# The end of an attention item: its addition, its copies of the reciprocal sums and GpSimd's three operations queued behind the next parts

## The chip, the cores and the metric

The kernel runs on one core of a Trainium2 chip. The metric is the device time of one execution in microseconds. The profile names the engines PE (TensorE's matmuls), PEld (its weight loads), DVE (VectorE), ACT (ScalarE), POOL (GpSimd) and SP (SyncE, which issues the DMAs here).

## The reference

One layer over 1024 latent tokens and 256 context tokens, width 1024, in fp32:

```python
x = macaron half-step SwiGLU(x)                  # every sub-layer with RMSNorm, shift, scale and gate
o_na  = neighbourhood attention(q, k, v, ...)    # 8 heads of 64; 8 x 16 window of a 64-wide grid + 256 context keys
o_mla = latent attention(q, k, v)                # 8 heads; 1024 latent + 256 context keys
y = g_na * (o_na @ w_o_na) + g_mla * (o_mla @ w_o_mla)
x = residual(x, y @ w_out)
x = macaron half-step SwiGLU(x)
```

Each attention is a softmax over scores, times the values:

```python
s = jnp.einsum('bqhd,bkhd->bhqk', q * q.shape[-1] ** -0.5, k).astype(jnp.float32)
p = jax.nn.softmax(s, axis=-1).astype(v.dtype)
return jnp.einsum('bhqk,bkhd->bqhd', p, v)
```

The neighbourhood attention adds a relative bias to its local scores, and puts local and context scores into one softmax.

## The kernel before

The change lies in the attention, which takes 1347 to 1757 us of the profiled execution. It is a list of 64 items, `todo`: 32 neighbourhood items (8 heads x 4 column blocks, `NaItem`), then 32 MLA items (8 heads x 4 blocks of 256 queries, `MlaItem`). Item n has 256 queries of one head. An fp32 operand of a product is kept as a pair, a rounded high half and the rest, so that a product is two or three matmuls.

For one item:

- `scores` multiplies queries by keys into PSUM banks of the kind "s" (tile `bs`). DVE adds the bias or copies, with the maximum (L1802 and L1777), and reduces the maxima (L1809, MLA L1909). ACT's exponential (L1811, MLA L1913) works in place and leaves the sums; DVE takes their reciprocal (L1815, MLA L1917). With an odd item, `widen` (L1769, POOL) spreads the reciprocals of this item and of the even one before it over a tile, `rope` in the profile.
- `values` gives the parts: three in a neighbourhood item (local, context, edge), five in an MLA item. A part transposes its exponentials on PE into a bank of the kind "m" (tile `bm`), ACT casts them to the high half (L1835, MLA L1939), DVE subtracts for the low half (L1836, MLA L1940). What is returned, `w`, are the part's matmuls with the values into the item's bank of the kind "v" (tile `bv`, columns 0 to 255). There are two "v" banks, so item n+2 writes the bank of item n.
- The `w` of the last part ends with `head_out`. A matmul with the values gives 128 rows, of which two blocks of 64 are to be added. In an even item, PE first transposes the widened reciprocals into columns 256 to 511 of the same bank, for this item and for the next: ACT copies them to `rb` (L1749) and to `other`, which the odd item takes as its `rb` (L1750). Then ACT copies one block to `o` (L1753), DVE adds the other (L1754), POOL multiplies by `rb` (L1755), casts (L1757) and subtracts (L1758) for the pair in `ona` or `omla`.

The loop over n makes a part, appends its `w` to `pending`, runs a share of the exponentials and reciprocals of an earlier item (`soft`), some steps of the scores of item n+3 (`ahead`), and the oldest `w` once more than two are pending (`LAG`). The matmuls, transposes and loads (helpers at L120, L132, L154 and L157) keep the order in which the program is written. The instructions of `head_out`, `turned`, `part` and `scores` on ACT, DVE and POOL go through no helper, and the framework's scheduler places them; each engine then runs its queue in that order. The small tiles `t`, with `o` and `rb` in them, come from a pool of 12 buffers in turn.

Of the kernel before, what the change touches and what calls it, by code (L numbers as in the profile page):

```python
# [12 lines left out]
ALU = mybir.AluOpType  # L13
# [25 lines left out]
def f32(ap):  # L39
    return ap.bitcast(F32)  # L40
# [3 lines left out]
def hybrid_block(ctx: ExitStack, tc: tile.TileContext, a: dict, out: bass.AP):  # L44
    nc = tc.nc
# [30 lines left out]
    def T2(dt=F32, n=512):  # L76
        return pools["t"].tile([P, n], dt, tag="t", name=nm("t"))
# [78 lines left out]
    def turn_(o, x, i):  # L156
        return pin(nc.tensor.transpose(o, x, i))  # L157
# [929 lines left out]
    o = len(plan.main)  # L1087
# [93 lines left out]
    o = d1_at + 4 * NP  # L1181
# [9 lines left out]
    for f, x in ups:  # L1191
        o = len(plan.main)
# [5 lines left out]
    for e in range(2):  # L1198
        for f in range(NF):
            o = len(plan.main)  # L1200
# [71 lines left out]
    def emit_cq(i, ci, x, bank):  # L1272

        t, q = x, T2()
        if bank:
            t = T2()
            act.copy(t, x)
        act.activation(q, t, AF.Square)
        if ci in sq:
            vec.tensor_tensor(sq[ci], sq[ci], q, op=ALU.add)  # L1280
        else:
            sq[ci] = q
        store(cqx[i, :, ci * 512:(ci + 1) * 512], t)
# [22 lines left out]
    for p in range(3):  # L1306
        punits.append(Unit(h2, [cq_src(2 * p), cq_src(2 * p + 1)],
                           lambda i, ci, x, bank, p=p: emit_cq(2 * p + i, ci, x, bank)))

    o = len(plan.main)  # L1310
# [147 lines left out]
    o = len(plan.main)  # L1458
# [5 lines left out]
    for x, (c, s, ts) in enumerate(sets):  # L1464
        o = len(plan.main)
# [239 lines left out]
    o = va_at  # L1705
# [8 lines left out]
    o = len(plan.main)  # L1714
# [3 lines left out]
    o = len(plan.main)  # L1718
# [3 lines left out]
    o = len(plan.main)  # L1722
# [4 lines left out]
    o = len(plan.main)  # L1727
# [9 lines left out]
    def head_out(pv, n, h, hi, lo, shape):  # L1737

        b, c = (0, 64) if h % 2 == 0 else (64, 0)
        t = T2()
        o, rb = t[b:b + 64, :256], t[b:b + 64, 256:512]
        if n % 2 == 0:
            for i in range(2):
                turn_(pv[:, 256 + i * P:256 + (i + 1) * P], wide(n)[:, i * P:(i + 1) * P], ident)
            other = held[0] = T2()
            nc.scalar.copy(rb, pv[0:64, 256:512])  # L1749
            nc.scalar.copy(other[b:b + 64, :256], pv[64:128, 256:512])  # L1750
        else:
            rb = held[0][b:b + 64, :256]
        nc.scalar.copy(o, pv[c:c + 64, :256])  # L1753
        nc.vector.tensor_tensor(o, o, pv[b:b + 64, :256], op=ALU.add)  # L1754
        nc.gpsimd.tensor_tensor(o, o, rb, op=ALU.mult)  # L1755
        o = shape(o)
        nc.gpsimd.tensor_copy(hi[b:b + 64], o)  # L1757
        nc.gpsimd.tensor_tensor(lo[b:b + 64], o, f32(hi[b:b + 64]), op=ALU.subtract)  # L1758

    sums, held = {}, [None]  # L1760

    def wide(n):

        return rope.rearrange("p a b -> p (a b)")[:, (n // 2) % 2 * 256:(n // 2) % 2 * 256 + 256]
# [18 lines left out]
    class NaItem:  # L1783
# [37 lines left out]
        def values(self):  # L1821
# [35 lines left out]
            def edge():  # L1857
                eh, el = edges[(h * 4 + j) % 2]
                turned(((0, 0), (1, 2)), eh, el)

                def w():
                    weigh(pv[0], vt(0), [x[:, 0:256] for x in (eh, el)], False, False)
                    weigh(pv[0], vt(3), [x[:, 128:384] for x in (eh, el)], False, True)
                    hi, lo = [o.rearrange("p (s r j c) -> p s r j c", s=2, r=8, j=4)[:, :, :, j, :] for o in ona[h // 2]]
                    head_out(pv[0], self.n, h, hi, lo, lambda t: t.rearrange("p (s r c) -> p s r c", s=2, r=8))
                return w
# [20 lines left out]
    class MlaItem:  # L1887
# [39 lines left out]
        def values(self):  # L1927
            hd, b, prl, prc, h = self.head, self.b, self.prl, self.prc, self.head.h
            pv = []

            def part(g):
                pb = PB("m")
                for x in range(2):
                    for s in range(2):
                        kb = 2 * g + x
                        src = prl[s][:, kb * P:(kb + 1) * P] if g < 4 else prc[:, s * 256 + x * P:s * 256 + (x + 1) * P]
                        turn_(pb[:, (2 * x + s) * P:(2 * x + s + 1) * P], src, ident)
                t = (T2(F32R), T2(F32R))
                nc.scalar.copy(t[0], pb)  # L1939
                nc.vector.tensor_tensor(t[1], pb, f32(t[0]), op=ALU.subtract)  # L1940

                def w():
                    if g == 0:
                        pv.append(PB("v"))
                    for x in range(2):
                        kb = 2 * g + x
                        vt = hd.v[:, kb * P:(kb + 1) * P] if g < 4 else hd.kvc[:, 512 + x * P:512 + (x + 1) * P]
                        weigh(pv[0], vt, [y[:, x * 256:(x + 1) * 256] for y in t], kb == 0, kb == 9)
                    if g == 4:
                        hi, lo = [o[:, b * 256:(b + 1) * 256] for o in omla[h // 2]]  # L1950
                        head_out(pv[0], self.n, h, hi, lo, lambda t: t)
                return w

            return [lambda g=g: part(g) for g in range(5)]

    soft, started, todo, edges, pending = [], [], [], [], []
    AHEAD, LAG, EARLY = 3, 2, 2

    def start(n):

        if n < len(todo):
            it = todo[n]()
            started.append(it)
            yield from it.scores()
# [101 lines left out]
    for n in range(len(todo)):  # L2066
        ahead = chain(start(EARLY), start(AHEAD)) if n == 0 else start(n + AHEAD)
        if n in (last - 4, last - 2):
            fm.load(int(n == last - 2))
        if n in (last - 3, last - 1):  # L2070
            fm.split()
        parts = led_parts[n] if n in led_parts else started[n].values()
        many = len(parts)
        soft_n = list(soft)
        for x, part in enumerate(parts):
            pending.append(part())
            take = rare[n][x] if n in rare else -(-len(soft_n) // (many - x))
            for f in soft_n[:take]:
                soft.remove(f)
                f()  # L2080
            del soft_n[:take]
            for _ in range(5 // many if n else 3):
                next(ahead, None)
            if x in fill.get(n, ()):
                fm.step()
            if len(pending) > LAG:
                pending.pop(0)()
        for _ in ahead:
            pass
    while pending:  # L2090
        pending.pop(0)()
    while fm.left:
        fm.step()
    pinned[0] = False
# [48 lines left out]
    for d in range(KD):  # L2143
        o = len(plan.main)
# [37 lines left out]
    o = len(plan.main)  # L2182
# [13 lines left out]
    o = len(plan.main)  # L2196
# [67 lines left out]
    for j in range(4):  # L2264
        o = d2_at + 5 * NP + 2 * j
        for x, i in enumerate((-2, 0, 1)):
            plan.spread([lambda j=j, x=x: done2(j, x)], o + i, o + i + 1)
        o = e - 9 + j
        plan.spread([lambda j=j: done_half(4 + j, 1)], o, o + 1)
        o = e - 4 + j  # L2270
# [83 lines left out]
```

## Time and profile before

| | before |
|---|---|
| median of 3 runs | 2560.17 us (2557.73 to 2561.82) |
| profiled execution | 2559.68 us, span 2557.7 us, mean granted clock 0.998 |
| PE, DVE, ACT, POOL busy | 2527.3, 1936.3, 1259.2, 217.8 us |
| 1375.36 to 1462.02 us (neighbourhood items): PE, DVE, ACT, POOL | 86.24, 84.43, 81.50, 44.93 of 86.66 us |
| 1564 to 1716 us (MLA items) | 151.29, 128.05, 121.26, 36.91 of 152 us |
| copies `rb`, `other` and `o` (L1749, L1750, L1753) | 32, 32 and 64 of them, medians 363, 368 and 368 ns |
| addition (L1754) | 64, median 420 ns |
| POOL's product, cast, subtraction (L1755, L1757, L1758) | 64 each, means 732, 398 and 733 ns |

How to read it: the span runs from the first to the last instruction of one profiled execution. A row of the timeline has the start, the length, engine, line, operation, output and inputs, and in brackets how long the engine had stood and what ended that. Consecutive matmuls overlap in the pipeline, so the sum of their lengths is more than their distance. Releasers are inferred.

### The profile page before, as it was taken

To read this page: it belongs to the slowest core of one execution; us is meant where nothing else is said; L and a number is where in the kernel's file an instruction comes from. 1 tells how busy PE (TensorE), PEld (TensorE's weight loads), DVE (VectorE), ACT (ScalarE), POOL (GpSimd) and SP (SyncE) were. 2 spreads that over 40 slices of the span, in tenths; PEclk is the share of its full clock that TensorE was granted. 3 is DMA by queue.
4 is the path that set the end of the run, shared out by engine and by line. 5 is a ranking of instruction groups with operands and counts; after the bars stand their busy time and mean duration, and the time that the engine had idled before them with its cause. 6 is when DMAs were issued, how large, how long until landed. Compare 5 with 4: busy or idle time off the path is not lost. (4 is left out here: it accounts for less than half of the span.)

```text
span 2557.7 us, 38230 instructions
## 1 busy us (share of the span) xinstructions
PE 2527.3 (99%) x13416; PEld 2158.7 (84%) x13416; DVE 1936.3 (76%) x3629; ACT 1259.2 (49%) x2375; POOL 217.8 (9%) x372
## 2 busy tenths in 40 slices
PE   8999999999999999999999999999999999999998
PEld 6888888888998888889888999998888888888887
DVE  4789986887786577874568988887886888767777
ACT  5632223445654653433447987783266322233444
POOL 1000000001000000001003522221011000000003
PEclk9999999999999999999999999999999999999999
DMA  8455543943674666755978733207836445326724
GB/s 307 157 173 195 195 151 117 345 137 132 231 274 138 215 230 225 241 184 176 301 280 275 241 94 76 65 11 262 296 123 216 156 157 169 111 99 233 273 70 165
DMA packets 245760, 479.47 MB, mean 187 GB/s; under 512 B 30464, under 2 KB 71616, under 8 KB 245568
## 3 DMA queue, kind: packets, MB, share of 16 engines
q1 hardware_dynamic: 245568, 477.02, 55.4%
q8 instruction: 106, 1.74, 0.3%
q14 instruction: 86, 0.70, 0.1%
HBM read 348.93 MB, written 127.99 MB: 186 GB/s over the span
## 5 line engine op out<-in xcount | busy, mean ns | idle before, releaser
L120 ACT CAST xu<-t 128x512 fp32r<-128x512 f32 (+1 forms) x270 | 161.0, 601 | 494.4 <-DVE t L120 352.6
L154 PE MATMUL bm<-xu,xu 128*128 128x512 f32 (+2 forms) x1572 | 366.6, 386 | 0.0
L154 PE MATMUL bs<-xv,xu 128*128 128x512 f32 x1488 | 357.3, 389 | 0.3 <-DVE t L120 0.3
L154 PEld LDWEIGHTS bm<-xu,xu 128*128 128x128 f32 x1572 | 288.1, 188 | 56.7
L154 PE MATMUL bv<-xv,xu 128*128 128x512 f32 x1342 | 335.4, 389 | 0.0
L154 PEld LDWEIGHTS bs<-xv,xu 128*128 128x128 f32 x1488 | 279.1, 188 | 59.0 <-issue 1.1
L154 PEld LDWEIGHTS bv<-xv,xu 128*128 128x128 f32 x1342 | 251.8, 188 | 52.3
L154 PE MATMUL bs<-xv,xv 128*128 128x512 f32 x1086 | 265.8, 390 | 0.0
L120 DVE TENSOR_TENSOR xu<-xu,xu 128x512 fp32r<-128x512 f32 (+1 forms) x296 | 201.7, 686 | 55.2 <-ACT xu L120 54.9
L154 PEld LDWEIGHTS bs<-xv,xv 128*128 128x128 f32 x1086 | 203.0, 188 | 41.7
L154 PE MATMUL bs<-xu,xu 128*128 128x512 f32 (+1 forms) x972 | 226.2, 382 | 0.0
L120 DVE TENSOR_TENSOR t<-t,t 128x512 f32<-128x512 f32 (+2 forms) x278 | 185.1, 673 | 45.0 <-ACT t L120 36.0
L154 PE MATMUL bs<-w,w 96*128 96x512 f32 (+3 forms) x832 | 206.5, 367 | 4.7 <-DVE st L1802 4.0
L154 PEld LDWEIGHTS bs<-xu,xu 128*128 128x128 f32 x972 | 177.4, 188 | 35.7 <-issue 1.4
L120 POOL TENSOR_SCALAR st<-st 128x1 f32<-128x1 f32 (+1 forms) x66 | 33.5, 508 | 1887.4 <-ACT t L120 1869.2
L120 ACT CAST xv<-t 128x512 fp32r<-128x512 f32 x170 | 105.8, 622 | 169.8 <-PE bv L154 69.0
L120 DVE TENSOR_TENSOR xu<-t,xu 128x512 fp32r<-128x512 f32 (+1 forms) x270 | 179.0, 663 | 10.7 <-ACT xu L120 10.6
L154 PE MATMUL bm<-xv,xv 128*128 128x512 f32 x690 | 182.8, 390 | 0.0
L120 ACT CAST xu<-xu 128x512 fp32r<-128x512 f32 x218 | 132.7, 618 | 71.3 <-DMA xu<-in_wo 43.6
L120 DVE TENSOR_TENSOR xv<-t,xv 128x512 fp32r<-128x512 f32 x170 | 116.6, 686 | 65.6 <-ACT xv L120 56.5
L154 PE MATMUL bv<-t,w 128*128 128x256 f32 x896 | 150.9, 288 | 2.0 <-DVE t L1940 1.5
L154 PEld LDWEIGHTS bm<-xv,xv 128*128 128x128 f32 x690 | 129.2, 188 | 27.1 <-issue 0.4
(242 smaller groups left out, 4229.3 us busy)
## 6 DMA issues: line engine op xcount, KB each, us to landing
d<-t SPq DMA_DIRECT2D x366, 256.0 KB, 2.6
t<-d SPq DMA_DIRECT2D x274, 256.0 KB, 3.8
xu<-in_f1w SPq DMA_DIRECT2D x59, 512.0 KB, 4.2
xu<-in_f2w SPq DMA_DIRECT2D x58, 512.0 KB, 3.7
t<-in_wada SPq DMA_DIRECT2D x112, 256.0 KB, 5.1
xv<-in_f1w SPq DMA_DIRECT2D x44, 512.0 KB, 7.4
xu<-in_winT SPq DMA_DIRECT2D x38, 512.0 KB, 4.8
w<-d SPq DMA_DIRECT2D x32, 512.0 KB, 6.4
```

Source lines behind the costliest of these rows:

```text
L120: return lambda *x, **y: pin(f(*x, **y))
L154: return pin(nc.tensor.matmul(o, s, m, start=start, stop=stop, skip_group_check=open_group[0]))
```

## The change

`head_out` still has PE transpose the reciprocals and ACT copy `o`. The rest goes into a function `one` that is appended to a list, `late`; an even item appends the copy to `other` as a second entry. The loop takes one entry out of `late` after each new part, ahead of that part's share of exponentials. So the addition, the copy to `rb` (now behind the addition) and POOL's three operations are written behind the transposes, cast and subtraction of the next part, and the copy to `other` behind those of the part after that. What is left runs after the loop. The lines move: 1753 to 1752 (`o`), 1754 to 1755 (addition), 1749 to 1757 (`rb`), 1750 to 1765 (`other`), 1755, 1757 and 1758 to 1758, 1760 and 1761 (POOL); everything behind them by 7.

```diff
         t = T2()
         o, rb = t[b:b + 64, :256], t[b:b + 64, 256:512]
-        if n % 2 == 0:
+        even = n % 2 == 0
+        if even:
             for i in range(2):
                 turn_(pv[:, 256 + i * P:256 + (i + 1) * P], wide(n)[:, i * P:(i + 1) * P], ident)
             other = held[0] = T2()
-            nc.scalar.copy(rb, pv[0:64, 256:512])
-            nc.scalar.copy(other[b:b + 64, :256], pv[64:128, 256:512])
         else:
             rb = held[0][b:b + 64, :256]
         nc.scalar.copy(o, pv[c:c + 64, :256])
-        nc.vector.tensor_tensor(o, o, pv[b:b + 64, :256], op=ALU.add)
-        nc.gpsimd.tensor_tensor(o, o, rb, op=ALU.mult)
-        o = shape(o)
-        nc.gpsimd.tensor_copy(hi[b:b + 64], o)
-        nc.gpsimd.tensor_tensor(lo[b:b + 64], o, f32(hi[b:b + 64]), op=ALU.subtract)
+
+        def one():
+            nc.vector.tensor_tensor(o, o, pv[b:b + 64, :256], op=ALU.add)
+            if even:
+                nc.scalar.copy(rb, pv[0:64, 256:512])
+            nc.gpsimd.tensor_tensor(o, o, rb, op=ALU.mult)
+            x = shape(o)
+            nc.gpsimd.tensor_copy(hi[b:b + 64], x)
+            nc.gpsimd.tensor_tensor(lo[b:b + 64], x, f32(hi[b:b + 64]), op=ALU.subtract)
+
+        late.append(one)
+        if even:
+            late.append(lambda: nc.scalar.copy(other[b:b + 64, :256], pv[64:128, 256:512]))
...
             pending.append(part())
+            if late:
+                late.pop(0)()
...
     while pending:
         pending.pop(0)()
+    while late:
+        late.pop(0)()
```

PE and SP run the same instructions in the same order before and after. ACT's queue at the end of an even MLA item (the one whose copies start at 1597.68 us in the profile), before; COPY on L1749, L1750 and L1753 are `rb`, `other` and `o`, CAST a part's high half, ACTIVATE an exponential, and the numbers in the names tell buffers and uses apart:

```order
L1913 ACTIVATE xu_16906,st_16904<-xu_16906,st_16903 128x1024
L1749 COPY t_17074<-bv_16960 64x256
L1750 COPY t_17077<-bv_16960 64x256
L1753 COPY t_17074<-bv_16960 64x256
L1939 CAST t_17090<-bm_17085 128x512
L1913 ACTIVATE t_16907,st_16904<-t_16907,st_16903 128x256
L1939 CAST t_17110<-bm_17105 128x512
L1939 CAST t_17129<-bm_17124 128x512
L1939 CAST t_17151<-bm_17146 128x512
```

and after, where L1752, L1757 and L1765 are `o`, `rb` and `other`:

```order
L1920 ACTIVATE xu_16906,st_16904<-xu_16906,st_16903 128x1024
L1752 COPY t_17074<-bv_16960 64x256
L1946 CAST t_17084<-bm_17079 128x512
L1920 ACTIVATE t_16907,st_16904<-t_16907,st_16903 128x256
L1946 CAST t_17109<-bm_17104 128x512
L1757 COPY t_17074<-bv_16960 64x256
L1765 COPY t_17077<-bv_16960 64x256
L1946 CAST t_17129<-bm_17124 128x512
L1946 CAST t_17151<-bm_17146 128x512
```

`o` stands straight behind the exponential, and the two other copies stand behind the casts of two parts.

DVE's queue at the same place, before (TENSOR_SCALAR copies scores with their maximum, the TENSOR_TENSOR that writes 128x512 is a part's low half, L1754 the addition):

```order
L1777 TENSOR_SCALAR xu_17040,st_17036<-bs_17065 128x512
L1777 TENSOR_SCALAR xu_17040,st_17036<-bs_17095 128x512
L1754 TENSOR_TENSOR t_17074<-t_17074,bv_16960 64x256
L1940 TENSOR_TENSOR t_17091<-bm_17085,t_17090 128x512
L1777 TENSOR_SCALAR xu_17041,st_17036<-bs_17115 128x512
L1940 TENSOR_TENSOR t_17111<-bm_17105,t_17110 128x512
```

and after, where the addition is L1755:

```order
L1784 TENSOR_SCALAR xu_17040,st_17036<-bs_17065 128x512
L1784 TENSOR_SCALAR xu_17040,st_17036<-bs_17094 128x512
L1947 TENSOR_TENSOR t_17085<-bm_17079,t_17084 128x512
L1755 TENSOR_TENSOR t_17074<-t_17074,bv_16960 64x256
L1947 TENSOR_TENSOR t_17110<-bm_17104,t_17109 128x512
L1784 TENSOR_SCALAR xu_17041,st_17036<-bs_17115 128x512
```

The addition has changed places with the low half of the part that follows.

ACT's queue at the end of an even neighbourhood item (its copies start at 1414.27 us in the profile), before; `xu<-bm` is the cast of an edge part, `xu,st` an exponential:

```order
L1749 COPY t_14152<-bv_14097 64x256
L1750 COPY t_14155<-bv_14097 64x256
L1753 COPY t_14152<-bv_14097 64x256
L1835 CAST xu_13012<-bm_14163 128x2x128
L1835 CAST t_14175<-bm_14177 128x512
L1811 ACTIVATE xu_14113,st_14117<-xu_14113,st_14116 128x640
L1835 CAST t_14201<-bm_14203 128x512
L1811 ACTIVATE xu_14114,st_14117<-xu_14114,st_14116 128x640
L1753 COPY t_14224<-bv_14170 64x256
```

and after:

```order
L1752 COPY t_14152<-bv_14097 64x256
L1842 CAST xu_13012<-bm_14157 128x2x128
L1842 CAST t_14174<-bm_14176 128x512
L1818 ACTIVATE xu_14113,st_14117<-xu_14113,st_14116 128x640
L1757 COPY t_14152<-bv_14097 64x256
L1765 COPY t_14155<-bv_14097 64x256
L1842 CAST t_14201<-bm_14203 128x512
L1818 ACTIVATE xu_14114,st_14117<-xu_14114,st_14116 128x640
L1752 COPY t_14224<-bv_14169 64x256
```

The two copies have moved from the front, ahead of `o`, to behind the first exponential. On DVE the same place reads, before:

```order
L1777 TENSOR_SCALAR xu_14114,st_14115<-bs_14112 128x256
L1754 TENSOR_TENSOR t_14152<-t_14152,bv_14097 64x256
L1809 TENSOR_REDUCE st_14116<-st_14115 128x2
L1836 TENSOR_TENSOR xu_13012<-bm_14163,xu_13012 128x2x128
L1815 RECIPROCAL st_13979<-st_14051 128x2
L1836 TENSOR_TENSOR t_14176<-bm_14177,t_14175 128x512
```

and after:

```order
L1784 TENSOR_SCALAR xu_14114,st_14115<-bs_14112 128x256
L1843 TENSOR_TENSOR xu_13012<-bm_14157,xu_13012 128x2x128
L1816 TENSOR_REDUCE st_14116<-st_14115 128x2
L1755 TENSOR_TENSOR t_14152<-t_14152,bv_14097 64x256
L1822 RECIPROCAL st_13979<-st_14051 128x2
L1843 TENSOR_TENSOR t_14175<-bm_14176,t_14174 128x512
```

The reduction of the maxima (TENSOR_REDUCE) stood behind the addition; now it stands behind the edge part's subtraction (`xu<-bm,xu`), and the addition behind it. In the first pair of items, ACT's queue reads, after:

```order
L1752 COPY t_13128<-bv_12919 64x256
L1842 CAST t_13133<-bm_13135 128x512
L1818 ACTIVATE xu_13045,st_13049<-xu_13045,st_13048 128x640
L1818 ACTIVATE xu_13046,st_13049<-xu_13046,st_13048 128x640
L1757 COPY t_13128<-bv_12919 64x256
L1818 ACTIVATE xu_13089,st_13093<-xu_13089,st_13092 128x640
L1842 CAST t_13164<-bm_13166 128x512
L1818 ACTIVATE xu_13090,st_13093<-xu_13090,st_13092 128x640
L1765 COPY t_13131<-bv_12919 64x256
L1752 COPY t_13188<-bv_13110 64x256
```

There `other` (L1765) stands behind four exponentials; before, both copies stood ahead of `o` here as well.

More of the change, by code (lines that the diff above doesn't have):

```diff
@@ L1954, in values @@
             return [lambda g=g: part(g) for g in range(5)]
-    soft, started, todo, edges, pending = [], [], [], [], []
+    soft, started, todo, edges, pending, late = [], [], [], [], [], []
     AHEAD, LAG, EARLY = 3, 2, 2
```

## The prediction

> **What bounds the kernel now.** I read the page first, then the busy time by stretch, then the waits of the attention stretch, and last the timeline at the ends of single items. The page's first part:
>
> ```profile
> PE 2527.3 (99%) x13416; PEld 2158.7 (84%) x13416; DVE 1936.3 (76%) x3629; ACT 1259.2 (49%) x2375; POOL 217.8 (9%) x372
> ```
>
> PE has work for all but 30 us of the 2557.7 us span, so the order of the other engines can only pay through PE's stalls. The busy time by stretch (window, its length, then PE, PEld, DVE, ACT, POOL, granted clock, DMA share, GB/s) for the steady part of the neighbourhood items and of the MLA items:
>
> ```profile
> 1375.36:1462.02 86.66, 86.24 (x683) 84.91 (x682) 84.43 (x308) 81.50 (x199) 44.93 (x77) 1.00 0.76 247
> 1564.00:1716.00 152.00, 151.29 (x1073) 139.26 (x1072) 128.05 (x383) 121.26 (x276) 36.91 (x63) 1.00 0.19 50
> ```
>
> The two stages differ. In the neighbourhood stage DVE (84.43 of 86.66) and ACT (81.50) are as full as PE: whatever lengthens a loop through these three sets the pace. In the MLA stage ACT and DVE have a fifth and a sixth of the time free, and only the order inside an item can hurt. From the waits of 1340 to 1760 us (engine, line and what it waited for: total, times, longest):
>
> ```profile
> DVE t L1754 <- ACT t L1753: 16.3, 21, 1.3
> ```
>
> The item's addition stands in DVE's queue and waits for the copy of o; all that follows it on DVE waits too. In the MLA items it reaches PE. One end of an even item:
>
> ```profile
> 1597.68 0.36 ACT L1749 COPY t<-bv 64x256 f32<-64x256 f32 x1
> 1598.44 0.36 ACT L1753 COPY t<-bv 64x256 f32<-64x256 f32 x1
> 1598.82 0.58 ACT L1939 CAST t<-bm 128x512 fp32r<-128x512 f32 x1
> 1598.83 0.42 DVE L1754 TENSOR_TENSOR t<-t,bv 64x256 f32<-64x256 f32 x1 [0.85 <-ACT t L1753]
> 1599.44 0.69 DVE L1940 TENSOR_TENSOR t<-bm,t 128x512 fp32r<-128x512 f32 x1 [0.18 <-ACT t L1939]
> 1599.74 0.28 PE L154 MATMUL bv<-t,w 128*128 128x256 f32 x1
> 1600.19 0.63 PE L154 MATMUL bv<-t,w 128*128 128x256 f32 x3 [0.16 <-DVE t L1940]
> 1601.81 0.65 PE L154 MATMUL bv<-t,w 128*128 128x256 f32 x4
> 1603.43 0.64 PE L154 MATMUL bv<-t,w 128*128 128x256 f32 x4
> ```
>
> ACT does the two copies of the reciprocal sums (from 1597.68), then o, then the cast of a part; DVE adds, then subtracts that part's low half, ready at 1600.13; PE, which had started that part's four matmuls at 1599.74, needs the low half for the second and stands. The four end at 1600.82, 1.08 us after their start, where the four at 1601.81 took 0.65: 0.43 us lost. Three other even ends, the first and the last of the steady row among them, and that of item 60:
>
> ```profile
> 1532.93 0.95 PE L154 MATMUL bv<-t,w 128*128 128x256 f32 x4
> 1566.48 0.87 PE L154 MATMUL bv<-t,w 128*128 128x256 f32 x4
> 1717.03 0.85 PE L154 MATMUL bv<-t,w 128*128 128x256 f32 x4
> 1733.03 0.28 PE L154 MATMUL bv<-t,w 128*128 128x256 f32 x1
> 1733.61 0.62 PE L154 MATMUL bv<-t,w 128*128 128x256 f32 x3 [0.30 <-DVE t L1940]
> ```
>
> The same four matmuls take 0.95, 0.87 and 0.85 (0.30, 0.22 and 0.20 lost), and 1.20 at item 60 (0.55 lost). From 1532.93 to 1717.03 there are twelve even ends: the first, five of the 0.43 kind and six of the 0.2 kind, so 0.30 + 5 x 0.43 + 6 x 0.21 = 3.7 us, and with item 60 about 4.3 us.
>
> **The change in the MLA items.** The order of ACT now has o straight behind the exponential, then the part's cast, then another exponential and cast, and only then the two copies; DVE has the part's subtraction ahead of the addition. So the cast moves from 1598.82 to 1598.06, by the 0.76 us of the two copies, and the subtraction starts when it ends, at about 1598.65, and ends near 1599.35: 0.4 us before PE starts the four matmuls. The stall goes. What is late next: the addition (0.42) follows at 1599.35, the copies follow it at about 1599.8 and end near 1600.55; behind them on ACT waits the cast of the next but one part, whose low half PE wants for the second of the four matmuls at 1603.43. Its cast and subtraction (0.58 and 0.69) end at about 1601.85. That cover is 1.5 us, so I cost the copies at nothing here; the multiplication on POOL starts some 0.8 us later, and POOL (36.91 of 152 busy) has room for it. PE's matmuls of the item after next now wait for the second copy, since the bank that it reads comes free later, but in MLA the bank's next user is a whole item away. Gain 4.3 us; if only half of each stall went it would be 2.1, and these are its bounds.
>
> **The change in the neighbourhood items.** One pair of items, at the end of an even one:
>
> ```profile
> 1414.27 0.36 ACT L1749 COPY t<-bv 64x256 f32<-64x256 f32 x1
> 1415.04 0.36 ACT L1753 COPY t<-bv 64x256 f32<-64x256 f32 x1
> 1415.43 0.43 DVE L1754 TENSOR_TENSOR t<-t,bv 64x256 f32<-64x256 f32 x1
> 1415.89 0.16 DVE L1809 TENSOR_REDUCE st<-st 128x2 f32<-128x4 f32 x1
> 1416.08 0.42 DVE L1836 TENSOR_TENSOR xu<-bm,xu 128x256 fp32r<-128x256 f32 x1
> 1416.49 0.67 DVE L1836 TENSOR_TENSOR t<-bm,t 128x512 fp32r<-128x512 f32 x1
> 1416.17 0.84 ACT L1811 ACTIVATE xu<-xu,st 128x640 f32<-128x640 f32 x1
> 1417.00 0.58 ACT L1835 CAST t<-bm 128x512 fp32r<-128x512 f32 x1
> 1417.29 0.71 PE L154 MATMUL bv<-t,w 128*128 128x256 f32 x4
> 1417.46 0.85 ACT L1811 ACTIVATE xu<-xu,st 128x640 f32<-128x640 f32 x1
> 1418.42 0.36 ACT L1753 COPY t<-bv 64x256 f32<-64x256 f32 x1
> 1418.81 0.37 ACT L1835 CAST xu<-bm 128x256 fp32r<-128x256 f32 x1
> 1420.14 0.83 ACT L1811 ACTIVATE xu<-xu,st 128x640 f32<-128x640 f32 x1 [0.47 <-DVE st L1809]
> 1424.05 0.84 ACT L1811 ACTIVATE xu<-xu,st 128x640 f32<-128x640 f32 x1
> ```
>
> From the first exponential of an item (1416.17) to that of the next (1420.14) and the one after (1424.05) it takes 3.97 and 3.91 us. At the second ACT stood 0.47 us for DVE's reduction, so DVE closes the loop. The two copies stood ahead of o, in time in which ACT would otherwise have waited for that reduction. Now they stand between the exponential and the next cast, and the reduction stands behind the subtraction of the edge part (the order shows: subtraction, reduction, addition, where it was addition, reduction, subtraction). The new loop of an even half, step by step from the starts above: exponential to cast 0.83, the two copies 0.77 (1414.27 to 1415.04), cast to second exponential 0.46, that to o 0.96, o to the edge part's cast 0.39, that cast 0.37, its subtraction 0.41 (1416.08 to 1416.49), reduction to exponential 0.19 (1415.89 to 1416.08): 4.38 us against 3.97, 0.41 more. The odd half has no copies; there the subtraction (0.41) takes the addition's slot (0.46) ahead of the reduction: 0.05 less. Together 0.36 us per pair. PE's idle time in the stretch is 0.42 us in eleven pairs, so PE has nothing to give and the loop's time is PE's time. Items 4 to 26 are twelve such pairs: 12 x 0.36 = 4.3 us lost. The bounds are nothing (if DVE catches up within the pair) and the whole 0.77 per pair, 9.2 us.
>
> The first pair differs. There the second copy comes behind three more exponentials and a cast:
>
> ```profile
> 1361.24 0.72 PE L154 MATMUL bv<-t,w 128*128 128x256 f32 x4
> 1362.86 0.38 PE L154 MATMUL bv<-t,w 128*128 128x256 f32 x1
> 1363.59 0.63 PE L154 MATMUL bv<-t,w 128*128 128x256 f32 x3 [0.34 <-DVE st L1809]
> 1362.71 0.84 ACT L1811 ACTIVATE xu<-xu,st 128x640 f32<-128x640 f32 x1
> 1363.66 0.37 ACT L1753 COPY t<-bv 64x256 f32<-64x256 f32 x1
> ```
>
> The copy reads the bank that PE's matmuls at 1361.24 (item 2) write again, so they wait for it. It now follows the exponential at 1362.71, which itself comes 0.38 earlier without the copy ahead: copy at about 1363.3, done at 1363.7. PE stands 2.5 us; of this the stall of 0.6 at 1362.86 was there anyway, and some of the rest is made up in the next pairs' waits. I take 1.5 us lost, between 0.5 and 2.5. In the other pairs the second copy ends some 1.6 us behind the exponential, at about 1417.75 on the old scale, where PE wants the bank at 1417.29 (the row above): a wait of up to 0.5 us that lies beside the loop's own 0.41 and not on top of it, as PE then reaches its next score matmuls when DVE does.
>
> **The rest.** The order on PE and SP is the same as before, so no load moves past another. POOL does the widening of an odd item's sums behind that item's products rather than between two of them; the rope transposes of PE that read it are several us away, so nothing.
>
> **The sum.** Of the profiled execution's 2559.68 us: -4.3 + 4.3 + 1.5 = +1.5, 2561.2. That execution lies 0.49 under the median of the runs, 2560.17, so the forecast for the median is 2561.7; the rivals' times below are on the median too. A difference of 0.2% (5.1 us) is about what a measurement of this kernel can tell from none; this is inside it.
>
> **The rivals.** First, slower: the copies lie wholly on the neighbourhood loop. For it: DVE at 84.43 of 86.66, and a second copy that PE itself waits for. Price: 12 x 0.77 = 9.2 in place of 4.3, so -4.3 + 9.2 + 1.5 = +6.4: 2566.6. It decides from 0.66 us per pair on ((5.1 + 4.3 - 1.5) / 12). Against it: ACT's wait of 0.47 shows room in one half.
>
> Second, the clock. Just ahead of the first pair PE stood twice, the second time for 1.95 us:
>
> ```profile
> 1353.32 0.50 PE L154 MATMUL bs<-w,w 128*128 128x256 f32 x2 [1.95 <-DVE st L1802]
> 1354.00:1356.00 2.00, 1.92 (x8) 1.93 (x9) 1.96 (x10) 1.11 (x4) 0.00 (x0) 0.63 1.01 388
> 1356.00:1358.00 2.00, 2.00 (x12) 2.00 (x11) 1.57 (x8) 0.37 (x1) 0.00 (x0) 0.51 1.05 405
> ```
>
> In the 4 us behind it the granted clock (third figure from the end) was 0.63 and 0.51: 2 x 0.37 + 2 x 0.49 = 1.7 us of PE's work lost. The new stall of 2.5 us could do the same again: +1.5 + 1.7 = +3.2, 2563.4. [...]
>
> Third, better: DVE makes up the 0.36 within each pair and only the first pair pays: -4.3 + 0.5 to 1.5, about -3.3: 2556.9. To be faster by over 5.1 us it would need the neighbourhood pairs to gain as well, where PE stands only 0.42 us.
>
> Fourth, the change does not do what it says: the copies wait for the addition at the head of ACT's queue, the casts behind them wait too, and PE's stall in the MLA items comes back one part later. Then the gain is gone: +4.3 + 1.5 = +5.8, 2566.0. Against it the cover of 1.5 us above.
>
> **How the numbers follow.** The forecast's case gets 0.39, the first rival 0.22, the clock 0.13, the better case 0.18, the last 0.08. Faster by over 0.2%: half of the better case, 0.09, for gains that I have not seen. Slower by over 0.2%: the first and fourth rivals, 0.30, and 0.03 for the clock together with a dearer loop: 0.33. Within: 0.58. The range reaches from the better case's side with all stalls gone and the first pair at 0.5 (-3.8: 2556.4) to the first rival with the clock (+8.1: 2568.3): 2556 to 2568.
>
> **What would show it.** Right: no MLA stall at even ends, so the four matmuls of 1599.74 take 0.65 everywhere; exponential to exponential about 4.4 and 3.85 in the neighbourhood pairs, 8.2 for a pair; a stall of about 2.5 us at item 2's first matmuls into its bank, waiting for the second copy. Wrong: pairs still at 7.9 (then 2557), or at 8.6 (then 2567); MLA stalls at even ends that stay; a clock under 1 behind 1364 us.

## The result

The changed kernel takes 2566.11 us (median of 9 runs, 2565.55 to 2566.98) against 2559.89 us of the kernel before beside it: ratio 1.0023, 95% interval 1.0014 to 1.0031, so slower by 3.6 to 7.9 us. The forecast was 2561.7, the range 2556 to 2568. The time lies in the range and near the first rival's 2566.6, but it was put together differently, as shown below. The profiled execution took 2566.62 us, with a span of 2564.5.

The page's first part of the changed kernel:

```profile
PE 2531.9 (99%) x13416; PEld 2160.3 (84%) x13416; DVE 1939.5 (76%) x3629; ACT 1267.9 (49%) x2375; POOL 218.2 (9%) x372
```

and its busy time by stretch for the two steady stretches (columns as before):

```profile
1381.00:1468.00 87.00, 85.30 (x654) 81.52 (x652) 81.35 (x294) 80.72 (x191) 43.50 (x74) 1.00 0.72 233
1564.00:1716.00 152.00, 150.60 (x1066) 138.16 (x1065) 128.47 (x380) 122.02 (x274) 37.45 (x65) 1.00 0.22 56
```

In the neighbourhood stretch PE now stands 1.70 us of 87 where it stood 0.42 of 86.66. In the MLA stretch, where the forecast took PE's stalls away, it stands 1.40 us of 152 where it stood 0.71. These figures show where PE stalls, not how much it loses: at 1599.74 in the kernel before, the profile had 0.16 us of standing where four matmuls took 0.43 us longer.

PE runs the same 13416 matmuls in the same order in every kernel here, so a trace can be split matmul by matmul: by how much the same matmul starts later than in the trace of before, and how that lag grows over a stage. "Pair 0" is from 1357.9 to 1369.6 us of before, "pairs" on to 1462.2, "MLA" from 1533.3 to 1718.4, "end" on to 1741.6 (item 60 is in it). In stages that an experiment left as they were, the lag moves by 0.0 to 0.35 us, which is what one trace can tell; e5's pairs are the exception, told below. The 0.35 is e3's pair 0, and it comes with the last matmul of that stage. The MLA column starts inside the first even end's stall (1532.93); counted from the start of that stall, the changed kernel's +0.81 is +0.60, and e8, e1, e4 and e7 have +0.25, +0.26, -1.16 and -2.22.

| us | measured against before: ratio (interval) | pair 0 | pairs | MLA | end |
|---|---|---|---|---|---|
| changed kernel | 1.0023 (1.0014 to 1.0031) | +3.31 | +3.80 | +0.81 | -0.16 |
| the same again (e8) | 1.0031 (1.0019 to 1.0042) | +3.34 | +3.72 | +0.46 | -0.20 |
| e1, MLA items alone | 1.0002 (0.9993 to 1.0011) | -0.02 | -0.02 | +0.48 | -0.22 |
| e2, neighbourhood items alone | 1.0030 (1.0019 to 1.0042) | +3.33 | +3.61 | -0.04 | +0.01 |
| e3, all but pair 0 | 1.0018 (1.0010 to 1.0027) | +0.35 | +3.98 | +0.36 | -0.27 |
| e4, MLA, addition at once | 0.9997 (0.9988 to 1.0006) | -0.01 | 0.00 | -0.95 | -0.29 |
| e5, pair 0 alone | 1.0011 (1.0002 to 1.0020) | +3.31 | -0.83 | +0.10 | -0.01 |
| e6, copies at once, addition late | 1.0020 (1.0011 to 1.0029) | +0.15 | +2.86 | +1.61 | -0.04 |
| e9, e6 with the reduction first | 1.0013 (1.0004 to 1.0022) | +0.14 | +0.60 | +1.54 | -0.08 |
| e10, changed kernel with the reduction first | 1.0013 (1.0004 to 1.0021) | +3.32 | +0.51 | +0.40 | -0.24 |
| e7, e4 with the odd items' o late | 0.9991 (0.9982 to 1.0000) | -0.02 | +0.09 | -2.00 | -0.22 |
| e7 again (e11) | 0.9991 (0.9982 to 1.0000) | -0.02 | 0.00 | -1.58 | -0.21 |

Pair 0 in the changed kernel's timeline:

```profile
1362.26 0.37 ACT L1765 COPY t<-bv 64x256 f32<-64x256 f32 x1
1362.68 0.73 PE L154 MATMUL bv<-t,w 128*128 128x256 f32 x4 [2.29 <-ACT t L1765]
```

and its busy time and clock in the 4 us behind that:

```profile
1363.00:1365.00 2.00, 2.00 (x13) 2.00 (x12) 0.76 (x2) 2.00 (x5) 1.43 (x3) 0.63 0.93 332
1365.00:1367.00 2.00, 2.00 (x11) 2.00 (x10) 1.24 (x4) 0.63 (x3) 0.82 (x2) 0.52 0.13 48
```

PE stood 2.29 us for the second copy (2.5 were forecast), and then the granted clock was 0.63 and 0.52 for 4 us: by the clock alone 2 x 0.37 + 2 x 0.48 = 1.7 us of PE's work. The matmuls lost less: from 1363.47 to 1367.01 us fifteen steps from one matmul's start to the next take 3.3 us and the same fifteen 2.0 before (the step with the stall of before is left out), so 1.3 us.

A neighbourhood pair of the changed kernel (exponential, the copies to `rb` and `other`, then `o`, edge cast, edge subtraction, reduction, addition and the next item's exponential):

```profile
1419.65 0.84 ACT L1818 ACTIVATE xu<-xu,st 128x640 f32<-128x640 f32 x1 [0.51 <-DVE st L1816]
1420.60 0.37 ACT L1757 COPY t<-bv 64x256 f32<-64x256 f32 x1
1420.99 0.37 ACT L1765 COPY t<-bv 64x256 f32<-64x256 f32 x1
1422.81 0.37 ACT L1752 COPY t<-bv 64x256 f32<-64x256 f32 x1
1423.20 0.37 ACT L1842 CAST xu<-bm 128x256 fp32r<-128x256 f32 x1
1423.61 0.42 DVE L1843 TENSOR_TENSOR xu<-bm,xu 128x256 fp32r<-128x256 f32 x1 [0.23 <-ACT xu L1842]
1423.95 0.15 DVE L1816 TENSOR_REDUCE st<-st 128x2 f32<-128x4 f32 x1
1424.13 0.42 DVE L1755 TENSOR_TENSOR t<-t,bv 64x256 f32<-64x256 f32 x1
1424.13 0.83 ACT L1818 ACTIVATE xu<-xu,st 128x640 f32<-128x640 f32 x1
```

DVE stands 0.23 us for the edge cast, and the reduction and the exponential that waits for it come behind: 4.48 us between the exponentials, against 3.97 before. Over 24 items (from 1368.7 us of before) the even half takes 4.42 us on average and the odd half 3.86, together 8.29; before it was 3.85, 4.02 and 7.87.

An MLA pair, an even end and the odd end behind it:

```profile
1601.11 1.16 ACT L1920 ACTIVATE xu<-xu,st 128x1024 f32<-128x1024 f32 x1 [1.28 <-DVE st L1916]
1604.88 0.59 ACT L1946 CAST t<-bm 128x512 fp32r<-128x512 f32 x1
1605.57 0.69 DVE L1947 TENSOR_TENSOR t<-bm,t 128x512 fp32r<-128x512 f32 x1 [0.81 <-ACT t L1946]
1606.29 0.66 PE L154 MATMUL bv<-t,w 128*128 128x256 f32 x4
1606.29 0.42 DVE L1755 TENSOR_TENSOR t<-t,bv 64x256 f32<-64x256 f32 x1
1606.75 0.69 DVE L1947 TENSOR_TENSOR t<-bm,t 128x512 fp32r<-128x512 f32 x1
1609.74 1.15 ACT L1920 ACTIVATE xu<-xu,st 128x1024 f32<-128x1024 f32 x1 [1.13 <-DVE st L1916]
1614.13 0.69 DVE L1947 TENSOR_TENSOR t<-bm,t 128x512 fp32r<-128x512 f32 x1 [0.19 <-ACT t L1946]
1614.39 0.28 PE L154 MATMUL bv<-t,w 128*128 128x256 f32 x1
1614.88 0.62 PE L154 MATMUL bv<-t,w 128*128 128x256 f32 x3 [0.20 <-DVE t L1947]
```

At the even end the four matmuls take 0.66: the stall is gone, as forecast. At the odd end they take 1.11, from 1614.39 to 1615.50. The same four before:

```profile
1608.28 0.64 PE L154 MATMUL bv<-t,w 128*128 128x256 f32 x4
```

The stall has moved by one item. It is so along the whole stretch. PE lost 0.44 us at each of five even ends; in the changed kernel it loses 0.47 at the odd end behind each. It lost 0.23 at six others; behind five of them it loses 0.33. So the larger stalls kept their size, and the smaller ones grew by 0.1.

### The profile page after: what moved, and what is told of

The parts are those of the page before. It is cut to its first block, busy times and chain, and to the rows that moved or that the text cites. A ratio compares the mean times of both kernels' runs of the same rounds, so it can differ in the third digit from the quotient of the medians.

```text
span 2564.5 us, 38276 instructions
## 1 busy us (share of the span) xinstructions
PE 2531.9 (99%) x13416; PEld 2160.3 (84%) x13416; DVE 1939.5 (76%) x3629; ACT 1267.9 (49%) x2375; POOL 218.2 (9%) x372
## 5 line engine op out<-in xcount | busy, mean ns | idle before, releaser
L120 DVE TENSOR_TENSOR xu<-t,xu 128x512 fp32r<-128x512 f32 (+1 forms) x270 | 179.5, 665 | 10.7 <-ACT xu L120 10.6
L154 PEld LDWEIGHTS bv<-t,w 128*128 128x128 f32 x896 | 133.9, 190 | 22.0 <-DVE t L1947 6.7
```

The source lines that it names most:

```text
L120: return lambda *x, **y: pin(f(*x, **y))
L154: return pin(nc.tensor.matmul(o, s, m, start=start, stop=stop, skip_group_check=open_group[0]))
```

## The experiments

e1 to e5 use the changed kernel with a test on the item: where it holds, the item ends as before, the copies ahead of `o` and nothing late.

```diff
+        now = n < 32      # e1; e2: n >= 32; e3: n < 2; e5: n >= 2; e4: n < 32
+        if even and now:
+            nc.scalar.copy(rb, pv[0:64, 256:512])
+            nc.scalar.copy(other[b:b + 64, :256], pv[64:128, 256:512])
         nc.scalar.copy(o, pv[c:c + 64, :256])
...
-            if even:
+            if even and not now:
                 nc.scalar.copy(rb, pv[0:64, 256:512])
...
+        if now:
+            one()
+            return
         late.append(one)
```

**Where the time is: e1, e2, e3, e5.** e1 (the MLA items alone):

> Only the MLA items (32 to 63) end in the new way; the neighbourhood items end as before. By the prediction's terms the stalls at the even ends go and nothing takes their place: -4.3 us against before, about 2555.6. By the theory read from the changed kernel's trace, the even stalls go but the addition, which stood in DVE's idle time before, now stands on DVE's way to the next maximum's reduction, so the next exponential opens no earlier and the stall comes back at the odd ends: between -0.6 (item 60 alone) and +0.6 us, 2559.3 to 2560.5, with stalls of 0.2 to 0.5 us at odd ends.

2558.53 against 2558.40 us: no change that can be told, and by the trace +0.48 over the MLA items and -0.22 at the end. The prediction's -4.3 is excluded (the interval ends at -1.8 us); the second theory's number came out.

e2 (the neighbourhood items alone):

> Only the neighbourhood items (0 to 31) end in the new way; the MLA items end as before. By the prediction's terms +4.3 for the twelve pairs and +1.5 for the first pair: +5.8 us, 2565.7. By the theory from the changed trace: +3.8 for the pairs, and +3.3 for the first pair, of which about 1.3 is a second fall of the granted clock behind a stall of 2.3 us: +7 us less what the runs vary at the start, 2566 to 2567.

2566.14 against 2558.40, +4.9 to +10.7 by the interval. It carries all of the loss. Pair 0 took +3.33 and the pairs +3.61.

e3 (the changed kernel without pair 0):

> The changed kernel, but items 0 and 1 end as before. Against the changed kernel's 2566.1: by the prediction's terms -1.5 us (2564.6); by the theory from the trace -3.3 us (2562.8), with no wait of 2.3 us for the second copy and a granted clock of 1.00 from 1360 us on. If the clock fell for another reason than that wait, about -2 us with a clock under 1 still seen between 1362 and 1368 us.

2563.00 against 2558.40. The trace has no wait for the copy, and a full clock, in the stretch that had 0.63 in the changed kernel:

```profile
1363.00:1365.00 2.00, 1.66 (x12) 1.40 (x12) 1.89 (x7) 1.95 (x7) 0.10 (x1) 1.00 1.05 387
```

The time alone does not decide between -1.5 and -3.3: the ratio 1.0018 is 0.0005 under the changed kernel's first and 0.0013 under its second, 1.3 to 3.3 us. The lag of +0.35 in place of +3.31 does.

e5 (pair 0 alone):

> The kernel before, but items 0 and 1 alone end in the new way. By the prediction's term +1.5 us against before; by the trace of the changed kernel +3.3 us, 1.9 from the wait for the second copy (2.5 less the old stall of 0.6) and 1.3 from the granted clock, which should again be near 0.65 for 4 us behind the wait. If the clock stays at 1.00 there, +1.5 to +2.

2561.86 against 2558.73, +0.5 to +5.1 us. The wait and the fall of the clock are there with nothing else changed, in its timeline:

```profile
1362.10 0.96 PE L154 MATMUL bv<-t,w 128*128 128x256 f32 x4 [2.25 <-ACT t L1772]
```

and in its busy time and clock:

```profile
1363.00:1365.00 2.00, 2.00 (x11) 2.00 (x10) 0.17 (x1) 1.58 (x4) 1.68 (x3) 0.50 0.76 278
```

The lag is +3.31, of which the next pairs give 0.83 back: 2.5 us net. In the changed kernel, against e3, the net is 2.8 us at the end of the pairs (3.31 + 3.80 less 0.35 + 3.98).

**Why the MLA items gained nothing: e4, e7, e11.** My theory after the trace was that the addition had stood in DVE's idle time and now stands between the part's subtractions, on DVE's way to the next item's reduction. e4 leaves the addition at once, and only the copies of the sums and POOL's operations late:

```diff
         nc.scalar.copy(o, pv[c:c + 64, :256])
+        nc.vector.tensor_tensor(o, o, pv[b:b + 64, :256], op=ALU.add)

         def one():
-            nc.vector.tensor_tensor(o, o, pv[b:b + 64, :256], op=ALU.add)
```

> Neighbourhood items as before. In MLA items the addition stays straight behind the copy of o, ahead of the next part's subtraction; only the copies of the reciprocal sums and GpSimd's operations go behind the next parts. By the theory that the addition's place on DVE is what undid the gain, the next exponential opens about 0.4 us earlier in each pair, the even stalls go and the odd ones stay away or under 0.25 us: -3 to -4.3 us against before, 2555.6 to 2557. By the rival theory, that the MLA pair is paced by something else (GpSimd's later products, the copies ahead of the third cast), no gain: 2559.5 to 2560.5.

2557.43 against 2558.40: unclear in time (0.9988 to 1.0006), -0.95 by the trace in the MLA items and -0.29 at the end, about a third of what was expected. The first exponentials of two items, before, in the changed kernel and in e4, around an even end:

```profile
1594.32 1.15 ACT L1913 ACTIVATE xu<-xu,st 128x1024 f32<-128x1024 f32 x1 [1.14 <-DVE st L1909]
1602.96 1.15 ACT L1913 ACTIVATE xu<-xu,st 128x1024 f32<-128x1024 f32 x1 [1.08 <-DVE st L1909]
```

```profile
1592.26 1.15 ACT L1928 ACTIVATE xu<-xu,st 128x1024 f32<-128x1024 f32 x1 [1.28 <-DVE st L1924]
1600.74 1.16 ACT L1928 ACTIVATE xu<-xu,st 128x1024 f32<-128x1024 f32 x1 [1.28 <-DVE st L1924]
```

8.64 us before, 8.63 in the changed kernel (1601.11 to 1609.74 above), 8.48 in e4. The same ten even ends (1544 to 1703 us of before) are of two kinds, five each: 8.63 and 8.40 us before, 8.63 and 8.51 in the changed kernel, 8.49 and 8.36 in e4; the means are 8.52, 8.57 and 8.42. Across the odd ends it is 8.22 to 8.24 in all three. So the change shortened the way from exponential to exponential nowhere and lengthened it at half of the ends, and moving the addition back shortened it, against the changed kernel, by 0.15 at both kinds. The late copies and POOL's late operations, the expectation's rival, are in e4 as well, so they alone did not undo the gain. In the changed kernel the late copies also wait for the addition (0.31 us at 1606.75), and a later cast stands behind them; e4 ends this too, and what part of the 0.15 lies there on ACT is not separated. In e4 the addition runs while DVE waits for the cast:

```profile
1662.61 0.42 DVE L1758 TENSOR_TENSOR t<-t,bv 64x256 f32<-64x256 f32 x1
...
1663.29 0.69 DVE L1955 TENSOR_TENSOR t<-bm,t 128x512 fp32r<-128x512 f32 x1 [0.26 <-ACT t L1954]
```

What was left in e4 were stalls of about 0.2 and 0.3 us at the odd ends, where the part's cast stood behind `o`. e7 puts `o` and the addition of odd MLA items behind that cast too:

```diff
+        def front():
+            nc.scalar.copy(o, pv[c:c + 64, :256])
+            nc.vector.tensor_tensor(o, o, pv[b:b + 64, :256], op=ALU.add)
+        if even or now:
+            front()
         def one():
+            if not (even or now):
+                front()
```

> As the fourth run (MLA: addition at once, copies and GpSimd's operations late; neighbourhood items as before), but in odd MLA items the copy of o and the addition go behind the next part's cast too. There the cast stood behind o (0.39 us) at each odd end and PE lost 0.17 to 0.32 us. By the theory that this is what is left on PE's way in the MLA pairs, 2 to 2.7 us less than the fourth run: about -3.5 us against before. If the pair is paced by DVE's way to the reduction, the addition moved behind the subtraction costs 0.4 us there and nothing is gained: about -1 us.

2556.13 against 2558.73, ratio 0.9991 (0.9982 to 1.0000), with -2.00 us by the trace in the MLA items: 1.05 less than e4, where 2 to 2.7 less was expected by the one theory and no gain by the other. Mean exponential to exponential 8.35 and 8.21; the odd ends have lost their stall, and the even ends keep 0.16:

```profile
1599.68 0.80 PE L154 MATMUL bv<-t,w 128*128 128x256 f32 x4
...
1613.01 0.64 PE L154 MATMUL bv<-t,w 128*128 128x256 f32 x4
```

Run again:

> The seventh run once more, to see whether it is faster than the kernel before: -2.6 us again, by the trace -2.4 (the MLA items alone).

2556.61 against 2558.71, the same ratio and interval, -1.58 by the trace. Each interval ends at 1, so neither run alone shows in time that this version is faster than the kernel before. That both give the same 2 us and both traces a gain in the same stage speaks for it.

**What the neighbourhood pairs lose to: e6, e9, e10.** The prediction put the 0.36 us per pair down to the two copies standing between exponential and cast. e6 takes them from there, in all items:

```diff
         nc.scalar.copy(o, pv[c:c + 64, :256])
+        if even:
+            nc.scalar.copy(rb, pv[0:64, 256:512])
+            nc.scalar.copy(other[b:b + 64, :256], pv[64:128, 256:512])

         def one():
             nc.vector.tensor_tensor(o, o, pv[b:b + 64, :256], op=ALU.add)
-            if even:
-                nc.scalar.copy(rb, pv[0:64, 256:512])
```

> All items: o and both copies of the reciprocal sums at the item's end at once (o first), only the addition and GpSimd's operations behind the next part. By the theory that the neighbourhood pairs lost their 0.36 us to the two copies between exponential and cast on ACT, and the first pair to the late second copy, both losses go: within 1 us of before. If the late addition and the changed place of the reduction were the cause, the pairs still take 8.2 us: about +4 us. If it were the bank freed late, that is gone too and the time is that of before.

2564.05 against 2558.73: the theory fell. The pairs still lost 2.86 us. In its trace, at the end of an even item:

```profile
1417.37 0.37 ACT L1841 CAST xu<-bm 128x256 fp32r<-128x256 f32 x1
...
1417.78 0.42 DVE L1842 TENSOR_TENSOR xu<-bm,xu 128x256 fp32r<-128x256 f32 x1
...
1418.12 0.14 DVE L1815 TENSOR_REDUCE st<-st 128x2 f32<-128x4 f32 x1
1418.30 0.42 DVE L1758 TENSOR_TENSOR t<-t,bv 64x256 f32<-64x256 f32 x1
1418.30 0.83 ACT L1817 ACTIVATE xu<-xu,st 128x640 f32<-128x640 f32 x1
```

The subtraction starts when the edge cast ends (1417.74), and the reduction comes behind it. Before, the reduction stood behind the addition, which does not need the edge cast; now it stands behind the edge subtraction, which needs it. ACT starts that cast 0.39 us after `o` in the changed kernel, and 1.05 us after it here, since the copies stand between the two; so e6 moved the copies and did not take them out of the loop. The order on DVE was made by the scheduler when the addition was written later. e9 is e6 with DVE's reduction and edge subtraction kept in the order in which they are written:

```diff
-            nc.vector.tensor_reduce(n_, ...)
+            r_ = nc.vector.tensor_reduce(n_, ...)
+            if self.n >= 4:
+                pin(r_)
...
-                nc.vector.tensor_tensor(ol, src, f32(oh), op=ALU.subtract)
+                d_ = nc.vector.tensor_tensor(ol, src, f32(oh), op=ALU.subtract)
+                if len(blocks) == 2 and self.n >= 2:
+                    pin(d_)
```

> As the sixth run (copies at once, addition and GpSimd's operations late), but in the neighbourhood items the reduction of the maxima and the edge part's subtraction keep the order in which they are written, so that DVE's queue reads addition, reduction, subtraction as in the kernel before. By the new theory (the pairs lose because the reduction stands behind the edge subtraction, which waits for a cast that ACT reaches one operation after o) the 0.31 us per pair go: 3.5 to 4 us less than the sixth run's +5.3, +1.3 to +1.8 against before. By the rival (something else about the late addition or the freed bank), no change: +5.

2562.33 against 2558.71: +1.0 to +5.6 by the interval, where +1.3 to +1.8 was expected. By the trace the pairs' lag went from 2.86 to 0.60, by 2.3 us in place of 3.5 to 4, because e6's pairs had lost less than the changed kernel's. DVE's queue there:

```profile
1417.64 0.42 DVE L1758 TENSOR_TENSOR t<-t,bv 64x256 f32<-64x256 f32 x1
1418.09 0.16 DVE L1815 TENSOR_REDUCE st<-st 128x2 f32<-128x4 f32 x1
1418.28 0.42 DVE L1844 TENSOR_TENSOR xu<-bm,xu 128x256 fp32r<-128x256 f32 x1
```

The rest of e9's time is the +1.54 of its MLA items, which e6 has too. In e6's trace the addition waits for the last of the three copies, though of what they write it reads only `o`. Like the copies it reads the bank `bv`; which of the two makes it wait, the traces do not show:

```profile
1586.40 0.41 DVE L1758 TENSOR_TENSOR t<-t,bv 64x256 f32<-64x256 f32 x1 [0.87 <-ACT t L1755]
```

So `o` first brings nothing as long as the copies stand between it and the cast. Where the +1.5 comes from can be read at a smaller stall, in the exponential ahead of the copies and the cast behind them. Before, and then in e6:

```profile
1579.82 1.14 ACT L1913 ACTIVATE xu<-xu,st 128x1024 f32<-128x1024 f32 x1
1581.98 0.58 ACT L1939 CAST t<-bm 128x512 fp32r<-128x512 f32 x1
```

```profile
1583.99 1.14 ACT L1919 ACTIVATE xu<-xu,st 128x1024 f32<-128x1024 f32 x1
1586.39 0.59 ACT L1945 CAST t<-bm 128x512 fp32r<-128x512 f32 x1
```

At the six smaller stalls the cast starts 2.16 us after the exponential before and 2.40 in e6 and e9, and PE loses 0.52 in place of 0.23; at the five larger ones it is 2.38 and 2.28, and 0.40 in place of 0.44. Why the same three copies take longer in the new order in some items and less in others stays open.

e10 makes the same edit on the changed kernel itself:

> The changed kernel with the same order of DVE's queue in the neighbourhood items (addition, reduction, edge subtraction). If the reduction's place alone makes the pairs' loss, 3.5 to 4.5 us less than the changed kernel's +6 to +8: about +3.5 (first pair +3.1, the rest nothing). If the two copies between exponential and cast lengthen the loop by themselves, as the prediction had it, about half or more of the pairs' loss stays: +5.5 to +7.

2563.10 against 2558.71, ratio 1.0013, +1.0 to +5.4. The pairs' lag is +0.51 in place of +3.8; pair 0 keeps its +3.32. With the reduction first, the scheduler also put the copy to `rb` ahead of the exponential and `other` behind it. So only one copy is left between exponential and cast, and this run does not tell what two of them there would cost by themselves.

**The changed kernel again, e8:**

> The changed kernel once more, on the same chip and beside the same runs of the kernel before as these: +6 to +7 us. The first pair's part then is this less the third run's +4.6: 1.5 us by the prediction's term, 3.3 by the trace.

2566.93 against 2558.73, 1.0031 (1.0019 to 1.0042), with the same split as the first trace to 0.35 us per stage. Less e3's 1.0018 this is 3.3 us for pair 0, where the traces have 2.8 net; the two intervals by themselves leave it open.

## Why the prediction was right or wrong

**The bound: half right.** PE's stalls decide, and the neighbourhood stage is paced by DVE and ACT; that held. For the MLA stage I concluded from a fifth of free time on ACT and DVE that only the order inside an item hurts. But the way from one item's exponential through casts, subtractions, score copies and reduction to the next exponential also paced it: with the even stalls gone it kept its 8.63 us at the larger ends. PE's stall at the even ends was where PE waited for that way, and not a loss of its own.

**The MLA term, -4.3: wrong, and the largest error.** With the first even end, which the forecast counted in, it measured +0.25 to +0.6 in the items and -0.2 at the end (e1: +0.13 in time). The steps that I worked out came true one by one: the cast 0.73 us earlier at the larger ends (1.65 us after the exponential in place of 2.38; 0.5 earlier at the smaller ones), the subtraction done just ahead of PE, no stall at the even end. The step that failed is "what is late next": I followed the addition only to the next matmuls of the same item, found 1.5 us of cover, and did not follow DVE's queue on to the reduction. There the addition (0.42) now fills much of what the earlier cast had won, the exponential came no earlier (8.57 us on average against 8.52), and PE, without its stall at the even end, met it at the odd end. e4 and e7 show it by taking the addition, and then the odd `o`, off that way: from +0.60 to -1.16 and to -2.22, of the -3.7 forecast for these ends. The last 1.5 us are the stalls of about 0.16 that e7 keeps at the even ends; what makes them was not tested. The fourth rival had the outcome ("PE's stall comes back"), but through ACT's casts and one part later, not through DVE and one item later.

**Pair 0, +1.5: the mechanism right, the size not.** The wait for the second copy was 2.29 us (forecast 2.5). The clock rival, which I gave 0.13, came true in every trace with that wait (2.25 to 2.29 us in the changed kernel, e2, e5, e8 and e10), and makes the difference, with 1.3 us in the changed kernel's matmuls where the rival had 1.7: lag +3.3, net of the later pairs 2.5 (e5) to 2.8 (changed kernel against e3). The bound of 2.5 that I gave the term left the clock out.

**The pairs, +4.3: the size about right, the step wrong.** They lost 3.6 to 4.0 us. The intervals between exponentials came out near the forecast (4.42 and 3.86 us for 4.4 and 3.85), and the long sum of the even half had in it both the copies and the edge subtraction ahead of the reduction; but I charged the loss to the copies and in the odd half counted the subtraction only as taking the addition's slot. e6, with the copies elsewhere, still loses 2.86. Putting the reduction first takes 2.3 us from e6 (to 0.60, e9) and 3.3 from the changed kernel (to 0.51, e10). So the subtraction's place made most of it. What the two copies cost by themselves is not separated: e6 keeps them in the loop at another place, and e10 moves one of them.

**The rivals.** The first rival's 2566.6 is nearest to the time, but its reason (the whole 0.77 us of copies on each pair) is not what happened. By the traces, from 1357.9 to 1741.6 us, the changed kernel lags by 7.7 us and its repeat by 7.2: pair 0 +3.3, pairs +3.7 to +3.8, MLA items and end +0.1 to +0.4, and 0.1 between the stages. The forecast had 1.5, 4.3 and -4.3; +3.6 to +7.9 was measured in time. That the time still fell into the range is luck: its upper end was set for a dearer loop with the clock, and the time came up there because the MLA gain was missing.

## What to carry to other kernels

When a queue is reordered to end a stall, follow the moved instruction along its engine up to the next thing that opens a new item (here the reduction ahead of the exponential), not only to the consumer that stood; a stall can be the place where a longer loop is felt (0.44 us at the larger even ends before, 0.47 at the odd ends behind them in the changed kernel). An operation that runs while its engine waits can stop being free when it is moved (the addition: with it back in its place, in e4, an even end takes 0.15 us less than in the changed kernel, a part of which may lie with the late copies). When one step is written later, a scheduler may change the order of others: look at what now stands ahead of the instruction that everyone waits for (here the edge subtraction ahead of the reduction: the pairs lag 3.8 us in the changed kernel and 0.51 in e10). And look at the first item by itself: the late bank made PE stand 2.29 us there, and no later item of the attention made it stand more than 0.34.

## What the runs showed of the hardware

A single idle of PE of 2.25 to 2.29 us was followed by a fall of the granted clock in each of the five traces that show it (2.29 in the changed kernel, 2.26 in e2, 2.25 in e5, 2.27 in e8 and e10). The traces of before, e1, e3 and e4, without that idle, have 1.00 from 1360 to 1368 us. The 2 us windows above mix two values: in the changed kernel the clock is 0.50 for 3.4 us, beginning 0.8 us after PE's restart at 1362.68, and 1.00 on both sides:

```profile
1362.68:1363.50 0.82, 0.82 (x7) 0.82 (x8) 0.57 (x2) 0.80 (x3) 0.07 (x1) 1.00 1.09 391
1363.52:1366.90 3.38, 3.38 (x18) 3.38 (x16) 1.48 (x5) 2.01 (x6) 2.12 (x4) 0.50 0.45 165
1366.95:1369.00 2.05, 2.05 (x19) 2.05 (x19) 1.80 (x7) 1.23 (x3) 0.00 (x0) 1.00 0.00 0
```

In e2, e5, e8 and e10 the 2 us windows behind the wait add up to the same 1.7 us by the clock alone. How much longer the matmuls take shows in two groups of four, in the changed kernel and then before:

```profile
1363.71 1.42 PE L154 MATMUL bs<-w,w 128*128 128x256 f32 x4
1365.78 1.05 PE L157 MATMUL bm<-ident,xu 128*128 128x128 f32 x4
```

```profile
1362.15 0.84 PE L154 MATMUL bs<-w,w 128*128 128x256 f32 x4
1364.05 0.60 PE L157 MATMUL bm<-ident,xu 128*128 128x128 f32 x4
```

The length of one idle does not decide alone. At the start of the attention PE stands 1.28 and 0.31 us before and in the changed kernel. In the changed kernel the clock is 0.50 from 1349.90 on, 1.4 us behind the second restart; before, it is still 1.00 there and falls only behind the next two idles, of 1.95 and 0.25 us. At the end of the attention PE stands once for 1.66 us in both, and the clock falls in neither. Before:

```profile
1348.80 0.50 PE L154 MATMUL bs<-w,w 128*128 128x256 f32 x2 [1.28 <-DVE st L1802]
1349.61 1.33 PE L154 MATMUL bs<-w,w 128*128 128x384 f32 x6 [0.31 <-DVE st L1802]
1349.90:1353.20 3.30, 1.47 (x10) 1.16 (x9) 0.84 (x5) 0.58 (x1) 0.00 (x0) 1.00 1.07 214
1758.88 2.57 PE L154 MATMUL bm<-xo,xu 128*128 128x512 f32 x10 [1.66 <-DVE xu L120]
1758.80:1768.00 9.20, 9.12 (x40) 7.57 (x41) 5.80 (x11) 1.16 (x3) 0.00 (x0) 1.00 1.03 383
```

In the changed kernel:

```profile
1347.66 0.50 PE L154 MATMUL bs<-w,w 128*128 128x256 f32 x2 [1.28 <-DVE st L1809]
1348.47 1.31 PE L154 MATMUL bs<-w,w 128*128 128x384 f32 x6 [0.31 <-DVE st L1809]
1349.90:1353.20 3.30, 1.66 (x6) 1.01 (x5) 1.73 (x9) 1.65 (x4) 0.00 (x0) 0.50 1.01 312
1765.49 2.56 PE L154 MATMUL bm<-xo,xu 128*128 128x512 f32 x10 [1.66 <-DVE xu L120]
1763.90:1768.00 4.10, 2.51 (x11) 2.10 (x12) 2.50 (x5) 1.14 (x2) 0.00 (x0) 1.00 0.95 329
```

From 1376 us to that last idle PE's idles, 0.34 us at most, left the clock at 1.00 in both.
